# One layer of a diffusion backbone: the attention's probabilities turned and scaled by one product with a diagonal, and the w_o splits ordered behind w_pa's

## The chip, the cores and the metric

The kernel runs on one core of one Trainium2 chip. The metric is the device time of one execution in microseconds. Before the change it is 1527.29 us (median of 3 runs, 1526.62 to 1529.53).

## The reference, cut to what matters

One layer: a half-step SwiGLU feed-forward, then two mixers side by side (a two-dimensional neighbourhood attention and a bidirectional gated DeltaNet), merged by per-channel gates, then a second feed-forward. There are 512 latent tokens, 256 context tokens, a model width of 1024 and 8 attention heads of width 64; everything is float32. The attention of one head over one row of the grid, and the merge:

```python
s = jnp.concatenate([s_loc.reshape(bsz, n_heads, width, n_loc), s_ctx], axis=-1).astype(jnp.float32)
p = jax.nn.softmax(s, axis=-1).astype(v.dtype)
...
return (jnp.einsum('bhwij,bhiwjd->bhwd', p_loc, v_win)
        + jnp.einsum('bhwn,bhnd->bhwd', p[..., n_loc:], v_ctx))
...
y = jax.nn.sigmoid(gate_a) * (o_a @ w_pa) + jax.nn.sigmoid(gate_b) * (o_b @ w_pb)
return y @ w_o
```

So the probabilities are exponentials divided by their row's sum, and they are multiplied with the values. The kernel needs them with the keys on the partitions for that product, so it turns each 128x128 block of them.

## The kernel before, in words

Large products are made of three passes of a rounded format: each operand is split into a high part (a cast on ScalarE, ACT, line 135) and a low part (a subtraction on VectorE, DVE, line 137), both in `split`; the product sums high by high, high by low and low by high (lines 190 to 192, and 209 in `down`). Weights come through a `Stream`: `fill` issues a load on SyncE's queue (line 172), makes the two parts with `split`, and keeps them in a queue; `get` fills a number of weights ahead and hands out the oldest. A stream may carry a table `behind`: for a weight named in it, the cast and the subtraction are issued after two given instructions of the same engines (`tc.issue_after`); it is an order on the engine, not an event to wait for.

The order of instructions on each engine is made by a planner in the tile framework: it runs through the program's order, but puts instructions ahead of others by costs and due times of its own. Each engine then works strictly in that order.

The attention (`attend`, lines 1228 to 1271) runs over 4 pairs of heads m, and in each over 4 column blocks b. For a block, 12 products make the scores of both heads into a PSUM tile `sc` (line 1240; two such tiles); DVE adds the bias (1242) and takes the negated maximum (1244); ACT makes the exponentials into `pr` with their sums `sm` (1248; two tiles of `pr`); DVE takes the reciprocal of the sums (1249). GpSimd (POOL) then multiplies the exponentials of each head with its inverse sums, 128x512 in place (1251). TensorE (PE) turns them, four transposes of 128x128 for each head into a PSUM tile `pt` (1255; two tiles), a set of four below; ACT copies each set into SBUF as `pT` (1257). Then 8 products of the values with `pT` sum into `po` (1266), an ordinary f32 product. At the start of each head pair the values are turned too (`att_values`, 1224 and 1225). Between the blocks stand pieces of other work: `between` calls at eight places the product of the other branch with w_pb (`gated`, lines 1282 to 1288, with 1302), and in the last pair fills four weights of w_o. `att_load` (1163 to 1180) loads and splits queries and keys of the next pair: the casts on ACT (1169), the subtractions on POOL (1170).

The merge (lines 1330 to 1335) runs over 8 column tiles m: it fills w_o up to a number that grows by one in every second step (1331); `gated` takes the weight of w_pa, with one weight ahead, loads the gate `gt` (1285) and makes 12 products; DVE gates the result (1333), POOL adds it to the other branch (1334), and `split` makes the two parts `yh` and `yl`. The product with w_o follows in `down` (209), for four token tiles over all eight tiles of w_o.

Of the kernel before, what the change touches and what calls it, by code (L numbers as in the profile page):

```python
# [10 lines left out]
F32 = mybir.dt.float32  # L11
F32R = mybir.dt.float32r
AF = mybir.ActivationFunctionType
ALU = mybir.AluOpType
# [4 lines left out]
P = 128  # L19
D = 1024  # L20
KT = D // P
# [37 lines left out]
def body(ctx, tc, I, out, dbg=None):  # L59
    nc = tc.nc  # L60
    V, S, G, T = nc.vector, nc.scalar, nc.gpsimd, nc.tensor
    dbg = dbg or {}

    def pool(name, side="left", space=None):
        kw = dict(name=name, bufs=1, reuse_waits="tile")
        if space is not None:
            kw["space"] = space
        else:
            kw["side"] = side
        g = tc.tile_pool(**kw)  # L70
        st = ExitStack()
        p = st.enter_context(g)
        return p, st.close
# [3 lines left out]
    def tl(p, shape, tag, bufs=1, dt=F32):  # L77
        uid[0] += 1
        return p.tile(list(shape), dt, name=f"{tag}_{uid[0]}", tag=tag, bufs=bufs)
# [11 lines left out]
    ident = ident_t[:]  # L91
# [40 lines left out]
    def split(src, hi, lo, behind=()):  # L132

        with tc.issue_after(behind[0]) if behind else nullcontext():
            S.copy(hi, src)  # L135
        with tc.issue_after(behind[1]) if behind else nullcontext():
            V.tensor_tensor(lo, src, hi.bitcast(F32), ALU.subtract)  # L137

    def to_u(tp, pp, xn, uh, ul, c0, scale, shift, tag="u32"):

# [13 lines left out]
    class Stream:  # L154
# [7 lines left out]
        def fill(self, n):  # L162
            while len(self.q) < n and self.i < len(self.srcs):
                src, p, bufs, rp, rb = self.srcs[self.i], self.wp, self.bufs, self.wp, self.bufs
                if isinstance(src, tuple):
                    if src[1] not in self.extra:
                        return
                    p, bufs, rp, rb = self.extra[src[1]]
                    src = src[0]
                c = src.shape[-1]  # L170
                raw = self.raw() if self.raw else tl(rp, [P, D], "wr", rb)
                nc.sync.dma_start(raw[:, 0:c], src)
                hi = tl(p, [P, D], "wh", bufs, F32R)
                lo = tl(p, [P, D], "wl", bufs, F32R)
                split(raw[:, 0:c], hi[:, 0:c], lo[:, 0:c], self.behind.get(self.i, ()))
                self.q.append((hi, lo))
                self.i += 1

# [4 lines left out]
    def mm3(ps, wh, wl, uh, ul, nk=KT):  # L183

        for k in range(nk):
            mm3k(ps, wh, wl, uh, ul, k, nk)
# [133 lines left out]
    def raw1():  # L320
        raws[0] += 1
        k = raws[0] % (5 if more[0] else 3)
        return tl(more[0], [P, D], "wr", 2) if k > 2 else tl(wx, [P, D], "wr") if k == 0 else tl(wp, [P, D], "wr", WB)
# [13 lines left out]
    def rows(w, ks):  # L337
        return [w[k * P:(k + 1) * P, :] for k in ks]
# [26 lines left out]
    def order1():  # L365
        t = lambda fs: [I["up1"][2 * f + j] for f in fs for j in range(2)]
        dn = lambda a, b: rows(I["dn1"], range(a, b))
        o = t(range(F0, F1)) + t(range(F1)) + t(range(F1, HF)) + dn(0, HF) + dn(0, HF - 2)
        o += t(range(HF, NF)) + dn(HF, NF - 4)
        n = len(o)  # L370
        o += dn(HF, NF - KL1)
        o = [(w, "x") if j % 3 == 2 else w for j, w in enumerate(o)]
        return o[:n] + [(w, "tail") for w in dn(NF - 4, NF)] + o[n:]
# [57 lines left out]
    ws = Stream(wp, order1(), WB, 1)  # L431
# [3 lines left out]
    for t in range(2):  # L435
        raw = raw1()
# [99 lines left out]
    def between(j):  # L536
        if j in FIN1:
            t = FIN1.index(j)
            u2(fc, pp, "x", t, finish1(fc, "x", t, accx[t]))
# [16 lines left out]
    src = [I["wab"] if n == "ab" else I["w" + n][m] if n in ("pa", "pb") else I["win"][WIN_IDX[(n, m)]] for n, m in order]  # L556
# [15 lines left out]
    gad = tl(dp, [8, P, NX], "gad")  # L572
    gbd = tl(dp, [8, P, NX], "gbd")

    ws = ws2
    names = iter(order)

    def win_w(name, m):
        assert next(names) == (name, m)
        return ws.get()  # L580
# [628 lines left out]
    oah = tl(np_, [P, 4, NX], "oah", 1, F32R)  # L1209
    oal = tl(np_, [P, 4, NX], "oal", 1, F32R)  # L1210
# [3 lines left out]
    na_, close_na = pool("na")  # L1214

    def att_values(w):

        wf = w[:].rearrange("p b r c -> p b (r c)")
        vw = tl(na_, [P, 4, 2, P], "vw", 2)
        for hb in range(2):  # L1220
            ps = tl(pg, [P, 4, P], "pt", 2)
            for q in range(4):
                b, kt = hb * 2 + q // 2, q % 2
                T.transpose(ps[:, q, :], wf[:, b, kt * P:(kt + 1) * P], ident)
            V.tensor_copy(vw[:, hb * 2:hb * 2 + 2].rearrange("p b k c -> p (b k) c"), ps[:])
        return vw

    def attend(m, qa, ka, kc, bias, w, between):
        vc = tl(na_, [P, 2, P], "vc", 2)
        nc.sync.dma_start(vc[:], vcd[m])  # L1230
        po = tl(pg, [P, 4, P], "po", 1)
        for b in range(4):
            pts = []

            sc = tl(pg, [P, 2, 512], "sc", 2)
            for o, k in ((0, [t.rearrange("p (r c) -> p r c", c=64)[:, :, NA_C0[b]:NA_C0[b] + 32] for t in ka]), (256, kc)):
                for j, (u, v) in enumerate(((0, 0), (0, 1), (1, 0))):
                    for i in range(2):
                        r = slice(i * 64, i * 64 + 64)
                        last = T.matmul(sc[:, i, o:o + 256], qa[u][r, b * P:(b + 1) * P], k[v][r], start=j == 0, stop=j == 2, tile_position=(i * 64, 0))  # L1240
            between(m, b, last.ins)
            V.tensor_tensor(sc[:, :, 0:256], sc[:, :, 0:256], bias[:, (0, 1, 1, 2)[b]], ALU.add)
            nm = tl(na_, [P, 2], "nm", 4)
            V.tensor_reduce(nm[:], sc[:], AX, ALU.max, negate=True)
            pr = tl(na_, [P, 2, 512], "pr", 2)
            sm = tl(na_, [P, 2], "sm", 4)
            for i in range(2):
                S.activation(pr[:, i], sc[:, i], AF.Exp, bias=nm[:, i:i + 1], accum_out=sm[:, i:i + 1])
            V.reciprocal(sm[:], sm[:])
            for i in range(2):  # L1250
                G.tensor_scalar(pr[:, i], pr[:, i], sm[:, i:i + 1], None, op0=ALU.mult)
            for i in range(2):
                pt = tl(pg, [P, 4, P], "pt", 2)
                for q in range(4):
                    T.transpose(pt[:, q, :], pr[:, i, q * P:(q + 1) * P], ident)  # L1255
                pT = tl(na_, [P, 4, P], "pT", 4)
                S.copy(pT[:], pt[:])
                pts.append(pT)
            if b == 0:
                vw = att_values(w)  # L1260

            for q in range(4):
                for i, pT in enumerate(pts):
                    f = slice(i * 64, i * 64 + 64)
                    vv = vw[:, b, q, f] if q < 2 else vc[:, q - 2, f]
                    T.matmul(po[f, b, :], vv, pT[:, q, :], start=(q == 0), stop=(q == 3), tile_position=(0, i * 64))  # L1266
        oa = tl(na_, [P, NX], "oa", 2)
        V.tensor_copy(oa[:].rearrange("p (r b c) -> p r b c", b=4, c=16), po[:].rearrange("p b (r c) -> p r b c", c=16))
        if "oa" in dbg:
            nc.sync.dma_start(dbg["oa"][:, m], oa[:])  # L1270
        split(oa[:], oah[:, m], oal[:, m])
# [10 lines left out]
    def gated(name, gd, m, oh, ol):  # L1282
        wh, wl = win_w(name, m)
        gt = tl(np_, [P, NX], "gt", 2)
        nc.sync.dma_start(gt[:], gd[m])
        ps = tl(pm, [P, NX], *PMB)
        mm3(ps[:], wh, wl, oh, ol, 4)
        return gt, ps
# [15 lines left out]
    for m in range(4):  # L1304
        if m == 3:
# [5 lines left out]
            wso = Stream(wp, [(w, k) if k else w for w, k in zip(rows(I["w_o"], range(KT)), ("b", "b", "b", "b", "o", "o", "o", ""))], WB, 1)  # L1311
# [16 lines left out]
    wo, close_wo = pool("wo", "right")  # L1328
    wso.extra["o"] = (wo, 3, np_, 2)
    for m in range(8):  # L1330
        wso.fill(min(4 + (m + 1) // 2, 7))
        gt, ps = gated("pa", gad, m, oah, oal)
        V.scalar_tensor_tensor(gt[:], gt[:], 1.0, ps[:], op0=ALU.add, op1=ALU.mult)
        G.tensor_tensor(yb[:, m], yb[:, m], gt[:], ALU.add)
        split(yb[:, m], yh[:, m], yl[:, m])
# [80 lines left out]
    src = [I["up2"][i] for i in range(2 * NH)]  # L1416
    ws = Stream(wp, [(w, key(j)) if key(j) else w for j, w in enumerate(src)], WB, 2)
# [134 lines left out]
    ws = Stream(wp, [(w, "d") if j % 6 > 1 else w for j, w in enumerate(rows(I["dn2"], range(NF)))], WB, 2)  # L1552
    ws.extra = {"d": (wd, 4, wp, WB)}
    raw = hs[NH:]
# [8 lines left out]
    for t in range(4):  # L1563
        h = tl(lp, [P, D], "h4", 2)
        n, m = (512, D) if t < 3 else (D // PIECES, 512)
# [125 lines left out]
```

## Time and profile before

| | |
|---|---|
| median of the runs | 1527.29 us (1526.62 to 1529.53) |
| the profiled execution | 1530.66 us, span 1528.8 us |
| granted TensorE clock, mean | 0.988 |
| busy: PE, DVE, ACT | 1462.6, 1050.0, 605.4 us |
| HBM read, written | 206.33 MB, 22.85 MB |

A row of a group reads: line, engine, operation, tile written and tiles read (moving operand first, weights second for a product), shapes, count, then busy time and mean duration in ns, then the idle time of the engine just before and what ended it. A row of the timeline reads: start, duration, engine, line, operation, tiles, count, and in brackets the idle time before it with what ended it. Times count from the start of the span. Matmuls are pipelined and their ends are modelled, so the spacing of starts tells more than the durations.

### The profile page before, as it was taken

How to read it: one execution, taken by the hardware profiler on the slowest of the kernel's cores; microseconds unless marked ns; L12 is line 12 of the kernel's file. 1: busy time of each engine (PE TensorE's matmuls, PEld its weight loads, DVE VectorE, ACT ScalarE, POOL GpSimd, SP SyncE). 2: the span in 40 equal slices, each digit the busy share in tenths (PEclk: the TensorE clock that was granted, in tenths of full speed). 3: DMA queues.
4: the chain of work that ended last, by engine and by line, in shares of the span. 5: the costliest groups of instructions: out<-in, count | busy, mean ns of one | idle time of the engine just before them, and what ended most of it. 6: DMA issues, size and time to landing. Idle time of an engine off the chain costs nothing.

```text
span 1528.8 us, 23646 instructions
## 1 busy us (share of the span) xinstructions
PE 1462.6 (96%) x9221; PEld 1258.7 (82%) x9221; DVE 1050.0 (69%) x1792; ACT 605.4 (40%) x1005; POOL 226.8 (15%) x224
## 2 busy tenths in 40 slices
PE   6999999999999999999996899999999999999997
PEld 4779988888888887889875778867678999998886
DVE  8765942597554587768777895576669699886426
ACT  5444221322222255546543444266416444344310
POOL 0000000000000011323301001366421022220001
PEclk9999999999999999999998999999999999999999
DMA  9665742667454334222476634283353143333422
GB/s 370 207 237 180 222 142 97 211 213 260 168 192 146 130 112 137 87 90 79 141 216 180 172 99 122 69 284 117 91 174 138 56 139 102 106 110 139 138 83 83
DMA packets 107586, 230.72 MB, mean 151 GB/s; under 512 B 34177, under 2 KB 47825, under 8 KB 107473
## 3 DMA queue, kind: packets, MB, share of 16 engines
q1 hardware_dynamic: 105312, 221.79, 44.7%
q10 hardware_dynamic: 1586, 5.32, 0.9%
q0 software_dynamic: 576, 2.10, 0.4%
q8 instruction: 72, 1.18, 0.3%
q14 instruction: 40, 0.33, 0.1%
HBM read 206.33 MB, written 22.85 MB: 150 GB/s over the span
## 4 chain that ended last, share of the span: by engine, by line
PE 76%; DVE 10%; DMA 7%; issue 3%; ACT 2%; POOL 2%; SPq 0%; DVEq 0%; ACTq 0%; POOLq 0%
PE ps L209 19%; PE ps L190 8%; PE ps L192 8%; PE ps L191 8%; PE pm L190 5%; PE pm L192 5%; PE pm L191 5%; PE pc L857 2%; PE ps L1478 2%; PE ps L1480 2%; PE ps L1479 2%; DVE wl L137 2%; PE po L1266 1%; DMA T<-rd 1%; PE pt L1255 1%
## 5 line engine op out<-in xcount | busy, mean ns | idle before, releaser
L137 DVE TENSOR_TENSOR wl<-wr,wh 128x1024 fp32r<-128x1024 f32 (+1 forms) x215 | 263.0, 1228 | 195.1 <-ACT wh L135 194.3
L135 ACT CAST wh<-wr 128x1024 fp32r<-128x1024 f32 (+1 forms) x215 | 217.8, 1018 | 333.4 <-PE ps L209 105.0
L192 PE MATMUL ps<-uxh,wl 128*128 128x512 f32 (+1 forms) x496 | 179.6, 363 | 2.2 <-DVE wl L137 2.2
L191 PE MATMUL ps<-uxl,wh 128*128 128x512 f32 (+1 forms) x496 | 179.3, 363 | 0.8 <-DVE uxl L137 0.8
L190 PE MATMUL ps<-uxh,wh 128*128 128x512 f32 (+1 forms) x496 | 179.6, 365 | 0.0
L279 DVE SCALAR_TENSOR_TENSOR adap<-wr,crow 128x1024 f32<-128x1024 f32 x112 | 136.8, 1221 | 38.5 <-DMA wr<-in_w_adaT_dram 37.1
L112 POOL TENSOR_TENSOR rs<-ve,mhalf 128x1 f32<-128x1 f32 (+2 forms) x46 | 50.4, 1099 | 744.6 <-DVE ve L108 735.4
L190 PE MATMUL pm<-uxh,wh 128*128 128x512 f32 x320 | 133.0, 416 | 4.1 <-ACT spill L609 2.1
L192 PE MATMUL pm<-uxh,wl 128*128 128x512 f32 x320 | 128.2, 401 | 0.7 <-DVE wl L137 0.7
L191 PE MATMUL pm<-uxl,wh 128*128 128x512 f32 x320 | 127.8, 399 | 0.0
L192 PEld LDWEIGHTS ps<-uxh,wl 128*128 128x128 f32 x496 | 93.7, 189 | 17.9 <-DVE wl L137 3.3
L191 PEld LDWEIGHTS ps<-uxl,wh 128*128 128x128 f32 x496 | 94.0, 189 | 14.9 <-DVE uxl L137 1.0
L190 PEld LDWEIGHTS ps<-uxh,wh 128*128 128x128 f32 x496 | 93.4, 189 | 14.3 <-issue 0.8
L190 PE MATMUL ps<-uch,wh 128*128 128x256 f32 x352 | 98.6, 280 | 0.0
L192 PE MATMUL ps<-uch,wl 128*128 128x256 f32 x352 | 98.3, 279 | 0.0
L191 PE MATMUL ps<-ucl,wh 128*128 128x256 f32 x352 | 98.2, 279 | 0.0
L209 PE MATMUL ps<-wh,hx 128*128 128x512 f32 x352 | 94.8, 389 | 0.0
L209 PEld LDWEIGHTS ps<-wh,hx 128*128 128x128 f32 x352 | 65.9, 188 | 13.6
L190 PEld LDWEIGHTS pm<-uxh,wh 128*128 128x128 f32 x320 | 61.6, 193 | 16.3 <-ACT spill L609 3.0
L192 PEld LDWEIGHTS pm<-uxh,wl 128*128 128x128 f32 x320 | 61.7, 193 | 14.8 <-DVE wl L137 1.5
L191 PEld LDWEIGHTS pm<-uxl,wh 128*128 128x128 f32 x320 | 61.6, 192 | 10.6
L190 PEld LDWEIGHTS ps<-uch,wh 128*128 128x128 f32 x352 | 66.1, 188 | 0.6
(411 smaller groups left out, 3438.7 us busy)
## 6 DMA issues: line engine op xcount, KB each, us to landing
wr<-in_w_adaT_dram SPq DMA_DIRECT2D x88, 512.0 KB, 4.7
wr<-in_up_dram SPq DMA_DIRECT2D x80, 512.0 KB, 4.2
wr<-in_dn_dram SPq DMA_DIRECT2D x58, 512.0 KB, 3.5
wr<-in_win_dram SPq DMA_DIRECT2D x52, 512.0 KB, 3.9
rb<-in_up_dram SPq DMA_DIRECT2D x18, 512.0 KB, 3.7
wr<-in_w_o_dram SPq DMA_DIRECT2D x8, 512.0 KB, 4.0
ac<-in_up_dram SPq DMA_DIRECT2D x6, 512.0 KB, 5.2
Dt<-gcd SPq DMA_DIRECT2D x12, 256.0 KB, 5.1
```

What stands on the lines that cost most here:

```text
L112: G.tensor_tensor(rs[:], ve[:], mhalf[:, 0:n], ALU.pow)
L135: S.copy(hi, src)
L137: V.tensor_tensor(lo, src, hi.bitcast(F32), ALU.subtract)
L190: T.matmul(ps, a, uh[:, k, :], start=(k == 0), stop=False)
L191: T.matmul(ps, a, ul[:, k, :], start=False, stop=False)
L192: T.matmul(ps, b, uh[:, k, :], start=False, stop=(k == nk - 1))
L209: T.matmul(banks[t][d][:, c0:c1], a[:, sl], b[:, d * 512 + c0:d * 512 + c1], start=first and j == 0, stop=last and j == 2)
L279: V.scalar_tensor_tensor(pr[:], raw[:], 1.0, crow, op0=ALU.mult, op1=ALU.mult, accum_out=col[:, c:c + 1])
L857: last[0] = T.matmul(*a, **k).ins
L1478: T.matmul(ps[:], a, uh[:, k], start=k == 0, stop=False)
L1479: T.matmul(ps[:], a, ul[:, k], start=False, stop=False)
L1480: T.matmul(ps[:], b, uh[:, k], start=False, stop=k == 3)
```

## The change

Two edits. In the attention, POOL's multiplication goes; DVE makes for each head a diagonal matrix of the inverse sums (identity times the column of inverse sums, 128x128), and the transpose of the exponentials becomes an ordinary f32 product of the exponentials, as weights, with that diagonal as the moving operand. In the merge, the fill of w_o is moved behind `gated` in the program's order, and every cast and subtraction of w_o from there on is to be issued after those of the w_pa weight loaded last; for that, `split` returns its two instructions and the stream keeps them.

```diff
     def split(src, hi, lo, behind=()):
 
         with tc.issue_after(behind[0]) if behind else nullcontext():
-            S.copy(hi, src)
+            a = S.copy(hi, src).ins
         with tc.issue_after(behind[1]) if behind else nullcontext():
-            V.tensor_tensor(lo, src, hi.bitcast(F32), ALU.subtract)
+            b = V.tensor_tensor(lo, src, hi.bitcast(F32), ALU.subtract).ins
+        return a, b
...
-                split(raw[:, 0:c], hi[:, 0:c], lo[:, 0:c], self.behind.get(self.i, ()))
+                self.last = split(raw[:, 0:c], hi[:, 0:c], lo[:, 0:c], self.behind.get(self.i, ()))
...
             V.reciprocal(sm[:], sm[:])
+
+            dg = tl(na_, [P, 2, P], "dg", 2)
             for i in range(2):
-                G.tensor_scalar(pr[:, i], pr[:, i], sm[:, i:i + 1], None, op0=ALU.mult)
+                V.tensor_scalar(dg[:, i], ident, sm[:, i:i + 1], None, op0=ALU.mult)
             for i in range(2):
                 pt = tl(pg, [P, 4, P], "pt", 2)
                 for q in range(4):
-                    T.transpose(pt[:, q, :], pr[:, i, q * P:(q + 1) * P], ident)
+                    T.matmul(pt[:, q, :], pr[:, i, q * P:(q + 1) * P], dg[:, i], start=True, stop=True)
...
     for m in range(8):
+        gt, ps = gated("pa", gad, m, oah, oal)
+
+        wso.behind = {j: ws.last for j in range(KT)}
         wso.fill(min(4 + (m + 1) // 2, 7))
-        gt, ps = gated("pa", gad, m, oah, oal)
         V.scalar_tensor_tensor(gt[:], gt[:], 1.0, ps[:], op0=ALU.add, op1=ALU.mult)
```

## The prediction

> **What bounds the kernel now.** I read the profile page first (busy shares, then the chain), then the table of windows for the two stretches that the change touches, then groups, waits and single rows inside them.
>
> ```profile
> PE 1462.6 (96%) x9221; PEld 1258.7 (82%) x9221; DVE 1050.0 (69%) x1792; ACT 605.4 (40%) x1005; POOL 226.8 (15%) x224
> ...
> PE 76%; DVE 10%; DMA 7%; issue 3%; ACT 2%; POOL 2%; SPq 0%; DVEq 0%; ACTq 0%; POOLq 0%
> ```
>
> TensorE is busy almost throughout and is three quarters of the chain that ends last; GpSimd, from which the change takes its work, is 2% of that chain.
>
> ```profile
> 994.00:1093.45 99.45, 91.86 (x729) 69.36 (x729) 63.42 (x91) 62.49 (x141) 63.75 (x41) 0.97 0.50 171
> 1093.45:1119.52 26.07, 23.30 (x98) 17.66 (x97) 21.35 (x24) 11.67 (x17) 9.79 (x7) 1.00 0.48 151
> 1028.00:1041.00 13.00, 10.33 (x61) 7.74 (x59) 5.77 (x9) 6.32 (x16) 6.74 (x5) 0.74 0.53 180
> 1060.02:1082.51 22.49, 22.49 (x169) 16.93 (x168) 17.19 (x24) 14.78 (x31) 14.93 (x9) 1.00 0.43 141
> ```
>
> The columns are stretch, length, busy PE, PE weight loads, DVE, ACT, POOL (with counts), granted clock, DMA share, GB/s. The first stretch is the attention (first scores to the first w_pa product), the second the merge. In the attention PE is idle for 99.45 - 91.86 = 7.6 us; DVE, ACT and POOL each have about a third of their time free. In 1060 to 1082, most of the last head pair, PE is never idle. Around 1034 there is the one bad place: the granted clock averages 0.74 there.
>
> **Edit 1, the turning.** Line 1251 (POOL) goes and line 1255 changes from a transpose to a product of the same shape, f32 by f32. The question is whether the shape sets the price or the mode.
>
> ```profile
> L1251 POOL TENSOR_SCALAR pr<-pr,sm 128x512 f32<-128x512 f32 x32 | 53.4, 1680 | 28.8 <-DVE sm L1249 23.4 <-PE pt L1224 5.3
> L1255 PE MATMUL pt<-ident,pr 128*128 128x128 f32 x128 | 21.4, 293 | 1.3 <-POOL pr L1251 1.3
> ```
>
> The same stretch of the windows for line 1266 alone:
>
> ```profile
> 994.00:1093.45 99.45, 23.21 (x256) 16.49 (x256) 0.97 0.50 171
> ```
>
> There are 16 blocks (4 head pairs by 4 column blocks). Line 1255 runs 8 times a block, 128 in all, and the trace has 128 records. Line 1266, an ordinary f32 product, also runs 8 times a block, 128 in all, and has 256. So a transpose is one pass of the array as recorded and an f32 product is two. The new line 1255 should have 256 records.
>
> What a record costs, by its start and the start of the next row:
>
> ```profile
> 1017.53 0.60 PE L1255 MATMUL pt<-ident,pr 128*128 128x128 f32 x4
> 1017.89 0.48 PE L191 MATMUL pm<-obl,wh 128*128 128x512 f32 x1
> ...
> 1018.89 0.66 PE L1255 MATMUL pt<-ident,pr 128*128 128x128 f32 x4
> 1019.48 0.54 PE L1266 MATMUL po<-pT,vw 128*64 128x128 f32 x5
> ```
>
> ```profile
> 970.48 1.05 PE L857 MATMUL pc<-r,Tt 128*128 128x128 f32 x8
> 971.37 1.06 PE L857 MATMUL pc<-S,qT 128*128 128x128 f32 x8
> 972.18 0.48 PE L190 MATMUL pm<-uxh,wh 128*128 128x512 f32 x1
> ```
>
> Four transposes take 0.36 us ahead of a 512-wide product and 0.59 us ahead of a product of another tile shape. Four f32 products of 128x128 by 128x128 (eight records, in the scan before) take 0.89 and 0.81, that is (0.89 + 0.81) / 16 = 0.106 us a record. The change adds 128 records: 128 x 0.106 = 13.6 us of PE. The bounds come from pairing the rows the other ways: 32 sets at 0.81 - 0.59 = 0.22 give 7.0, 32 at 0.89 - 0.36 = 0.53 give 17.0. I take 13.6, since both kinds of neighbour occur and the step per record is the same before both.
>
> The Trainium skill, "TensorE: Matmul & The Clock Gate", section Terms, says that transpose mode is four times faster for FP32; "Perfetto Trace Analysis", section Transposes, asks that logical transposes use the transpose and not a standard matmul. By that factor, an estimate from the page, each product would cost four times 0.09 us and the sum would be near +35 us; by that rule a set would take 1.44 us, and the scan's sets of 0.81 and 0.89 do not bear it out.
>
> **What hides it.** Nothing but PE's own idle time, since PE works in order. That time in the attention, by releaser:
>
> ```profile
> PE po L1266 <- ACT pT L1257: 4.0, 5, 1.9
> PE pt L1255 <- POOL pr L1251: 1.3, 2, 0.7
> PE pt L1224 <- DVE vw L1225: 0.8, 1, 0.8
> PE sc L1240 <- ACT pr L1248: 0.7, 1, 0.7
> ...
> PE sc L1240 <- POOL ka L1170: 0.2, 1, 0.2
> ```
>
> Only 1.5 us of it names POOL: 1.3 for the scaled probabilities, and 0.2 for a split (line 1170) queued behind them on POOL. Both should go. The scores wait for exponentials, not for POOL, so the 53.4 us taken from POOL are mostly time that nobody waits for.
>
> Behind 1.8 of the 4.0 us stands POOL indirectly: in the last two blocks there is no other work left and the sets come as late as POOL delivers them.
>
> ```profile
> 1088.28 0.54 PE L1266 MATMUL po<-pT,vw 128*64 128x128 f32 x5 [0.37 <-ACT pT L1257]
> ...
> 1090.68 0.43 PE L1266 MATMUL po<-pT,vw 128*64 128x128 f32 x2 [0.73 <-ACT pT L1257]
> ...
> 1092.43 0.54 PE L1266 MATMUL po<-pT,vw 128*64 128x128 f32 x5 [0.73 <-ACT pT L1257]
> ```
>
> With the diagonal ready within a microsecond of the reciprocal, the sets can be issued back to back and the copies of pT hide behind the next set; I give 1.5 of the 1.8 back. Late next is the copy after the last set.
>
> The rest of the 4.0 is the bad place at 1034:
>
> ```profile
> 1032.25 0.62 ACT L1169 CAST kah<-ka 128x512 fp32r<-128x512 f32 x1 [4.01 <-DMA ka<-kad]
> ...
> 1034.25 0.58 ACT L1257 COPY pT<-pt 128x512 f32<-128x512 f32 x1
> ```
>
> ```profile
> 1034.88 0.90 PE L1266 MATMUL po<-pT,vw 128*64 128x128 f32 x5 [1.88 <-ACT pT L1257]
> ...
> 1036.78 1.12 PE L1255 MATMUL pt<-ident,pr 128*128 128x128 f32 x4
> 1037.82 0.58 PE L1240 MATMUL sc<-kah,qah 64*128 64x256 f32 x2
> ```
>
> ACT waits 4.0 us at the head of its queue for the keys of the last head pair, with the pT copy queued behind; PE stands 1.9 us and then runs at half clock: a set takes 1.04 instead of 0.59. A mean clock of 0.74 over 13.00 us is half clock for 2 x 0.26 x 13.00 = 6.8 us, a loss of 3.4, of which the 1.9 us of standing take 0.9; so 2.5 us of work are lost besides the wait. The wait is for a DMA, not for POOL, and stays; the two sets that PE has just ahead of it grow by 0.8 us and eat into it, and the half clock may or may not follow. I take half of 1.9 + 2.5: 2.2 us. Given back in all: 1.5 + 1.5 + 2.2 = 5.2 us. The bounds are 0 and all idle time plus the half clock, 7.6 + 2.5 = 10.1.
>
> **The diagonal.** It adds two DVE operations a block, 32 in all, queued behind the reciprocal and ahead of the next block's bias add.
>
> ```profile
> L685 DVE TENSOR_SCALAR na<-na x7: 181/188/190, 690.7 to 699.0; 128x48 f32<-128x48 f32 x7
> ...
> L998 DVE COPY Y<-pi x6: 271/281/283, 833.1 to 951.7; 128x128 f32<-128x128 f32 x6
> ```
>
> Not in the trace before; between 0.19 (smaller, same operation) and 0.28 (same size, out of PSUM) each, so 6 to 9 us on DVE, 36 us of which are free in the stage. DVE also gains: beside POOL's operations its two-input subtractions take up to 1.75 us instead of 0.68 (a row of 1.75 is below). I cost it at nothing; if the cover were gone, each block's chain would be 0.4 to 0.6 us longer against 3.4 us (two of 1680 ns) that leave it with POOL.
>
> **Edit 2, the casts.** In the merge PE waits 2.7 us in all, for the low halves of w_pa:
>
> ```profile
> 1101.42 0.50 PE L192 MATMUL pm<-oah,wl 128*128 128x512 f32 x1 [0.95 <-DVE wl L137]
> ...
> 1114.18 0.50 PE L192 MATMUL pm<-oah,wl 128*128 128x512 f32 x1 [1.78 <-DVE wl L137]
> ```
>
> ```profile
> 1094.81 2.00 ACT L135 CAST wh<-wr 128x1024 fp32r<-128x1024 f32 x2
> 1098.54 1.14 ACT L135 CAST wh<-wr 128x512 fp32r<-128x512 f32 x2 [1.73 <-PE pm L191]
> ```
>
> ```profile
> 1095.88 2.36 DVE L137 TENSOR_TENSOR wl<-wr,wh 128x1024 fp32r<-128x1024 f32 x2 [0.26 <-ACT wh L135]
> ...
> 1111.17 0.69 DVE L1333 SCALAR_TENSOR_TENSOR gt<-gt,pm 128x512 f32<-128x512 f32 x1 [1.00 <-DMA gt<-gad]
> 1111.77 0.69 DVE L137 TENSOR_TENSOR yl<-yb,yh 128x512 fp32r<-128x512 f32 x1
> 1112.38 1.75 DVE L137 TENSOR_TENSOR wl<-wr,wh 128x512 fp32r<-128x512 f32 x1
> ```
>
> Rows of 1024 are w_o, rows of 512 w_pa. Two of w_o's splits run at 1094.8 to 1098.2, when ACT and DVE have nothing else: the next w_pa cast cannot start before 1098.54, because its buffer is still being read by PE. They delay nobody. The 1.78 us wait has no w_o split ahead of it at all, but the gate's DMA (1.00), a yl, and a subtraction stretched to 1.75. So binding w_o behind w_pa takes away little: the issue of the gate load ahead of w_o on SP may be worth a few tenths. Against that, two splits of 2.36 us on DVE leave an idle stretch for a busy one (21.35 of 26.07). Bounds -2.7 and +2.4; I take 0, because w_o's next use is after all eight w_pa products.
>
> **The sum.** 13.6 - 5.2 + 0 = +8.4 us. The profiled execution took 1530.66 (span 1528.8), 3.4 above the median of 1527.29; on it 1539.1, on the median 1535.7.
>
> **The rivals.**
> - No change: PE loses all its idle time. 13.6 - 10.1 - 2.7 = +0.8, 1528. For it: the idle time is there. Against: half of it follows a DMA, and single waits of this order at tile hand-overs return in any order of work. 0.14.
> - Faster: the second record of a product is nearly free, because its weight load or stream overlaps the first's in this mix of short products. It decides below 5.2 / 128 = 0.04 us a record; at 0.02 the sum is 2.6 - 5.2 = -2.6, at zero 1522. For it: no row has this product between po and score products. Against: 0.106 in the scan. 0.16.
> - The bound casts become the wait: DVE's 2.4 us land ahead of w_pa's subtractions. 8.4 + 2.4 = +10.8, 1538. For it: DVE at 82% in the merge. 0.13.
> - The rule of four passes: three more passes of 0.09 for 128 products, 35 - 5 = +30, 1557. As a mechanism it is that each of the two records takes twice the pass; the scan's rows speak against. 0.02.
> - The forecast, 0.55.
>
> **How the numbers follow.** A measurement of this kernel can tell about 0.2%, 3 us, from no change. Slower holds the forecast, the bound casts and the four passes, 0.70; same 0.14; faster 0.16. The range: upwards 17.0 for the records with 1.3 + 0.5 given back, about +15.5, so 1543; downwards the no-change case and the upper part of the faster one, 1525.
>
> **What would show it.** Line 1255 with 256 records and about 0.8 to 1.0 us a set; PE busy up by some 13 us in the attention, idle below 5; POOL near 63.75 - 53.4 = 10 us there; the last set's wait the only one of the tail; the w_o splits after w_pa's in the merge and that stretch near 26 us. I am wrong if line 1255 keeps 128 records or its records cost under 0.04 us, if the attention is not longer than 99.5 us, or if the merge shortens by over 2 us.

## The result and the profile after

The changed kernel takes 1541.65 us (median of 6 runs, 1537.77 to 1545.04). The kernel before, run beside it, takes 1527.22 us (6 runs, 1525.69 to 1529.53). The ratio is 1.009 with a 95% interval of 1.0071 to 1.0108: slower by 14.4 us. The forecast was 1535.7 with a range from 1525 to 1543, slower with a chance of 0.70.

One warning about the two profiles. The profiled execution of before took 1530.66 us, 3.4 above its median; that of after took 1537.77, the fastest of its six. So the two traces differ by 7.1 us where the medians differ by 14.4. The stages were therefore compared over several profiles of each kind, below.

The page of after, the busy times and the shares of the chain that ended last:

```profile
PE 1476.1 (96%) x9349; PEld 1275.0 (83%) x9349; DVE 1055.4 (69%) x1824; ACT 605.2 (39%) x1005; POOL 174.7 (11%) x192
...
PE 78%; DVE 11%; DMA 5%; issue 2%; POOL 1%; ACT 1%; SPq 0%; DVEq 0%; POOLq 0%; ACTq 0%
```

PE has 9349 - 9221 = 128 more records and 13.5 us more busy time; POOL has lost 32 instructions and 52 us. TensorE's share of the chain rose from 76% to 78%.

The windows of after for the attention, the merge, and the stretch from the first product with w_o to the first product of the last stage (the sums of seven products in the second feed-forward), with the columns of before:

```profile
992.07:1100.79 108.72, 104.91 (x857) 84.60 (x856) 69.11 (x123) 62.33 (x141) 9.82 (x9) 1.00 0.47 157
1100.79:1128.42 27.63, 23.68 (x98) 17.62 (x97) 23.69 (x25) 11.69 (x17) 11.40 (x7) 1.00 0.44 138
1128.42:1222.30 93.88, 92.47 (x609) 84.64 (x608) 69.61 (x110) 42.10 (x76) 13.67 (x14) 1.00 0.37 128
```

The attention grew from 99.45 to 108.72 us: 13.05 us more busy PE (91.86 to 104.91), less 3.8 us of idle time (7.6 to 3.8). The merge grew from 26.07 to 27.63. The third stretch became shorter; in the profile of before it is

```profile
1119.52:1217.10 97.58, 94.54 (x609) 86.17 (x608) 72.22 (x111) 42.03 (x76) 14.25 (x14) 0.98 0.35 122
```

that is 97.58 against 93.88 us. Keep this row in mind for the second edit.

The turning line of after, by source line:

```profile
L1258 PE MATMUL pt<-dg,pr x256: 270/275/377, 1000.2 to 1098.8; 128*128 128x128 f32 x128
```

256 records for 128 products, each of a transpose's length. PE's timeline in the third head pair shows what a set of four now takes, by its start and the start of the next row:

```profile
1042.44 1.16 PE L1258 MATMUL pt<-dg,pr 128*128 128x128 f32 x8
1043.53 0.38 PE L1241 MATMUL sc<-kah,qah 64*128 64x256 f32 x2
...
1048.39 1.16 PE L1258 MATMUL pt<-dg,pr 128*128 128x128 f32 x8
1049.30 0.48 PE L193 MATMUL pm<-obh,wl 128*128 128x512 f32 x1
...
1097.89 1.16 PE L1258 MATMUL pt<-dg,pr 128*128 128x128 f32 x8
1098.97 0.43 PE L1269 MATMUL po<-pT,vw 128*64 128x128 f32 x2
1099.78 0.54 PE L1269 MATMUL po<-pT,vw 128*64 128x128 f32 x5 [0.37 <-ACT pT L1260]
```

A set takes 1.09 us ahead of a product of another tile shape (before: 0.59) and 0.91 ahead of a 512-wide one, where the four single sets of after take 0.81 to 0.92. Before, the three sets ahead of a 512-wide product took 0.36, 0.41 and 0.42; the prediction shows the shortest, and this is the middle one:

```profile
1015.22 0.66 PE L1255 MATMUL pt<-ident,pr 128*128 128x128 f32 x4
1015.63 0.47 PE L191 MATMUL pm<-obl,wh 128*128 128x512 f32 x1
```

So a set costs about 0.50 us more before either neighbour, 32 times. The last two of the rows of after are the tail: the copy of the last set is now the only wait there, 0.37 us, where before three waits of 0.37, 0.73 and 0.73 stood in the last two blocks.

PE's waits in the attention of after:

```profile
PE sc L1241 <- ACT pr L1249: 1.6, 1, 1.6
PE pt L1225 <- ACT pT L1260: 1.3, 1, 1.3
PE pt L1258 <- DVE dg L1254: 0.5, 1, 0.5
PE po L1269 <- ACT pT L1260: 0.4, 1, 0.4
```

No wait names POOL any more. The 4.0 us of the value products (line 1266, now 1269) for `pT` are down to 0.4. One wait of 0.5 for the new diagonal has come, and two have grown: that of the scores for exponentials from 0.7 to 1.6, and that of the values' turning for `pT` from 0.3 to 1.3. In the merge DVE now does this:

```profile
1102.28 0.69 DVE L137 TENSOR_TENSOR oal<-oa,oah 128x512 fp32r<-128x512 f32 x1 [0.69 <-ACT oah L135]
1106.11 1.28 DVE L1338 SCALAR_TENSOR_TENSOR gt<-gt,pm 128x512 f32<-128x512 f32 x2 [3.14 <-PE pm L193]
1107.31 4.22 DVE L137 TENSOR_TENSOR wl<-wr,wh 128x512 fp32r<-128x512 f32 x3
```

DVE stands still for 3.14 us at the place where it made two subtractions of w_o before (2.36 us at 1095.88). The w_o parts come later, among w_pa's.

### The profile page after: what moved, and what is told of

Its sections match the earlier page's. It is cut to its first block, busy times and chain, and to the rows that moved or that the text cites. A ratio compares the mean times of both kernels' runs of the same rounds, so it can differ in the third digit from the quotient of the medians.

```text
span 1536.0 us, 23873 instructions
## 1 busy us (share of the span) xinstructions
PE 1476.1 (96%) x9349; PEld 1275.0 (83%) x9349; DVE 1055.4 (69%) x1824; ACT 605.2 (39%) x1005; POOL 174.7 (11%) x192
## 4 chain that ended last, share of the span: by engine, by line
PE 78%; DVE 11%; DMA 5%; issue 2%; POOL 1%; ACT 1%; SPq 0%; DVEq 0%; POOLq 0%; ACTq 0%
PE ps L210 19%; PE ps L191 9%; PE ps L193 9%; PE ps L192 9%; PE pm L191 5%; PE pm L193 5%; PE pm L192 5%; PE pc L858 3%; PE pt L1258 2%; PE ps L1485 2%; PE ps L1483 2%; PE ps L1484 2%; DVE wl L137 2%; PE po L1269 1%; DMA Dt<-gcd 1%
## 5 line engine op out<-in xcount | busy, mean ns | idle before, releaser
L191 PEld LDWEIGHTS ps<-uxh,wh 128*128 128x128 f32 x496 | 92.7, 188 | 14.4 <-issue 0.8
L193 PE MATMUL ps<-uch,wl 128*128 128x256 f32 x352 | 98.3, 279 | 0.0
L210 PEld LDWEIGHTS ps<-wh,hx 128*128 128x128 f32 x352 | 65.9, 188 | 13.6
```

What stands on the lines that cost most here:

```text
L191: T.matmul(ps, a, uh[:, k, :], start=(k == 0), stop=False)
L193: T.matmul(ps, b, uh[:, k, :], start=False, stop=(k == nk - 1))
L210: T.matmul(banks[t][d][:, c0:c1], a[:, sl], b[:, d * 512 + c0:d * 512 + c1], start=first and j == 0, stop=last and j == 2)
```

## The experiments

**Theory A**: the second record of each product is the loss, at a higher price in this mix of short products than in the scan; POOL's step gives a few microseconds back; the casts are worth little. **Rival B**: the bound casts in the merge are a substantial part of it. **Rival C**: the products themselves are cheap, and the loss comes from the other order that the planner makes, and from the diagonals on DVE. Times are medians; each ratio is to runs of the kernel before on the same chip.

### The first edit alone

```diff
+            dg = tl(na_, [P, 2, P], "dg", 2)
             for i in range(2):
-                G.tensor_scalar(pr[:, i], pr[:, i], sm[:, i:i + 1], None, op0=ALU.mult)
+                V.tensor_scalar(dg[:, i], ident, sm[:, i:i + 1], None, op0=ALU.mult)
...
-                    T.transpose(pt[:, q, :], pr[:, i, q * P:(q + 1) * P], ident)
+                    T.matmul(pt[:, q, :], pr[:, i, q * P:(q + 1) * P], dg[:, i], start=True, stop=True)
```

> Edit 1 alone, the fill of w_o where it was. Theory A (the second record of each f32 product is the price): +9 to +15 us over the kernel before, the attention about as long as with both edits, 108.7 us. Rival B (the bound w_o splits are the price): within 3 us of the kernel before. Rival C (the planner's new order around DVE's diagonals is the price): near the whole loss too, so this run does not tell A from C.

Measured: 1538.87 us against 1527.62, ratio 1.0075 (1.0056 to 1.0093), +11.2 us. Its windows for attention and merge:

```profile
993.83:1102.85 109.02, 104.94 (x858) 84.62 (x857) 69.14 (x123) 62.42 (x141) 9.82 (x9) 1.00 0.46 156
1102.85:1128.58 25.73, 23.30 (x98) 17.66 (x97) 21.36 (x24) 11.67 (x17) 9.90 (x7) 1.00 0.48 149
```

The attention is that of the whole change (108.72); the merge is that of before (26.07). Most of the loss is the first edit's, and the longer merge is the second's.

### The second edit alone

The diff is the second edit: `split` returns its two instructions, the stream keeps them, and the merge loop has the moved fill and the line `wso.behind = {j: ws.last for j in range(KT)}`.

> Edit 2 alone, the attention as before. A: -1 to +2 us, the merge 26 to 28 us long. B: +8 to +14 us.

Measured: 1526.02 us against 1527.62, ratio 0.9987 (0.9978 to 0.9996), -1.6 us. Its windows for attention, merge, the stretch behind it, and 40 us that begin 60 us into that stretch and reach a little past its end:

```profile
992.83:1091.33 98.50, 90.71 (x729) 68.69 (x728) 62.30 (x91) 62.60 (x141) 63.57 (x41) 0.98 0.52 173
1091.33:1118.96 27.63, 23.65 (x98) 17.65 (x97) 23.69 (x25) 11.57 (x17) 11.39 (x7) 1.00 0.43 139
1118.96:1212.80 93.84, 92.52 (x610) 84.69 (x609) 69.72 (x110) 42.16 (x76) 13.69 (x14) 1.00 0.37 128
1178.96:1218.96 40.00, 37.41 (x313) 36.63 (x311) 28.56 (x44) 20.56 (x36) 2.32 (x2) 1.00 0.19 65
```

and the same 40 us (60 to 100 us after the first product with w_o) of before:

```profile
1179.52:1219.52 40.00, 37.86 (x310) 37.66 (x309) 26.81 (x44) 18.14 (x34) 0.67 (x2) 0.96 0.23 79
```

The merge loses 27.63 - 26.07 = 1.6 us and the next stretch gains 97.58 - 93.84 = 3.7: the granted clock in the 40 us is 1.00 instead of 0.96, PE's wait for `y` (line 128) is 1.3 us instead of 2.1, and a wait of 0.8 for `uxl` (line 137) is gone. So rival B falls as the main cause: alone the second edit is a small gain, made of two opposite effects. What this experiment doesn't say is whether it is the move or the binding; see the move without the binding, below.

### The product alone, with the identity

```diff
-                    T.transpose(pt[:, q, :], pr[:, i, q * P:(q + 1) * P], ident)
+                    T.matmul(pt[:, q, :], pr[:, i, q * P:(q + 1) * P], ident, start=True, stop=True)
```

> The kernel before with one thing changed: the transposes are ordinary f32 products with the identity, GpSimd still scales. A: line 1255 has 256 records, 0.8 to 1.1 us a set, and the kernel is 12 to 19 us slower, more than with the whole change, since GpSimd's step is still in the chain of each block. C: 0 to 4 us, since nothing new is queued on DVE.

Measured: 1543.49 us against 1527.62, ratio 1.01 (1.0084 to 1.0116), +15.9 us. Its window of the attention:

```profile
993.20:1106.97 113.77, 108.83 (x858) 87.51 (x857) 64.48 (x91) 63.32 (x141) 61.07 (x41) 0.97 0.44 150
```

In the program nothing but the kind of instruction has changed, and POOL still scales; line 1255 has 256 records, a set takes 1.09 us ahead of a product of another tile shape, and the attention grows by 113.77 - 99.45 = 14.3 us. That is the price of 128 products for 128 transposes: 0.112 us each by the stage, 0.124 by the medians (0.100 to 0.138 by their interval). The planner's order of PE's work is not quite that of before (between the first two sets stand 4 score products instead of 8), and this price contains what that does.

### POOL's step left out

```diff
-            for i in range(2):
-                G.tensor_scalar(pr[:, i], pr[:, i], sm[:, i:i + 1], None, op0=ALU.mult)
```

> The kernel before without GpSimd's scaling, transposes kept (the division by the sums is left out of the attention). It prices what the change takes away: A expects -2 to -6 us, the idle time that names GpSimd, the tail and part of the half clock around 1034 us. If the step is worth nothing, within 1 us; if it is worth as much as it looks by its 53 us busy, below -10 us.

Measured: 1522.97 us against 1527.62, ratio 0.9969 (0.9957 to 0.9982), -4.65 us.

```profile
991.14:1086.87 95.73, 89.63 (x729) 67.44 (x729) 60.30 (x91) 62.52 (x141) 9.69 (x9) 0.98 0.54 178
```

The attention is shorter by 99.45 - 95.73 = 3.7 us, and POOL's busy time by 54 us. So this is all that the step on POOL costs when it goes without a replacement. It is not simply the waits that go: PE's idle time in the stage falls only from 7.6 to 6.1 us, and its busy time, with the clock at 0.98 instead of 0.97, by 2.2 us. The waits for POOL are gone and those of the value products for `pT` are 0.8 instead of 4.0, but two others have come in their place, of which before had 0.3 us:

```profile
PE pt L1224 <- ACT pT L1255: 2.6, 1, 2.6
PE pm L190 <- ACT spill L607: 2.6, 1, 2.6
```

With the product by the identity the sum closes: +15.9 - 4.65 = +11.25, and the first edit alone measured +11.2. Each of the three is known to 2 or 3 us only, so that it closes to a tenth is chance.

### The whole change again

No diff: the changed kernel, on the chip of the next three.

> The changed kernel once more, beside the others of this call. A: +9 to +16 us. The merge should again be 1.5 to 2 us longer than before (27.6 us) and the stretch from the first w_o product to the first product of the seven (93.9 us) 2 to 4 us shorter, as edit 2 alone showed; if the merge is back at 26 us, that reading was chance.

Measured: 1541.62 us against 1526.51, ratio 1.009 (1.0066 to 1.0113), +15.1 us. Its window of the attention, and 17 us early in it:

```profile
994.90:1106.47 111.57, 106.46 (x858) 85.79 (x857) 70.21 (x123) 62.44 (x141) 9.73 (x9) 0.98 0.45 153
...
1003.00:1020.00 17.00, 12.71 (x98) 10.43 (x98) 13.51 (x24) 11.35 (x27) 4.93 (x5) 0.90 1.01 376
```

The result stands, and so do the longer merge (27.62 us) and the shorter stretch behind it (93.81). The attention is 2.9 us longer than in the first profile of the same kernel: early in it PE waits 2.9 us for exponentials instead of 1.6, and the clock falls to 0.90. The 16 DMA engines are full here (1.01), but they were as full at the same place of the first profile, where the clock stayed at 1.00:

```profile
1000.00:1017.00 17.00, 13.87 (x117) 11.50 (x119) 13.83 (x25) 12.34 (x30) 4.95 (x5) 1.00 1.04 394
```

So what makes the difference is not shown, and one profile of this stage is worth no more than about 3 us.

### The first edit in the rounded format

On top of the first edit, the exponentials and the diagonal are tiles of the rounded format that the large products of this kernel use, so that the same product takes one pass:

```diff
-            pr = tl(na_, [P, 2, 512], "pr", 2)
+            pr = tl(na_, [P, 2, 512], "pr", 2, F32R)
...
-            dg = tl(na_, [P, 2, P], "dg", 2)
+            dg = tl(na_, [P, 2, P], "dg", 2, F32R)
```

> Edit 1 alone, but exponentials and diagonal in the rounded format that the large products use, so that the turning keeps DVE's diagonals and the order around them, and only the passes per product differ (the probabilities lose low bits). A: line 1257 has 128 records, 0.4 to 0.6 us a set, and the kernel is 1 to 6 us faster than before, near the run without the scaling. C (order, diagonals on DVE): still 8 us or more slower.

Measured: 1526.11 us against 1526.51, ratio 0.9999 (0.9988 to 1.0009), -0.4 us. Its window of the attention:

```profile
991.59:1089.20 97.61, 93.07 (x730) 72.97 (x729) 68.79 (x123) 62.53 (x141) 10.76 (x9) 0.95 0.50 175
```

and PE's timeline:

```profile
1021.28 0.66 PE L1257 MATMUL pt<-dg,pr 128*128 128x128 f32 x4
1021.78 0.44 PE L192 MATMUL pm<-obh,wl 128*128 128x512 f32 x1
...
1023.17 0.66 PE L1257 MATMUL pt<-dg,pr 128*128 128x128 f32 x4
1023.76 0.39 PE L1240 MATMUL sc<-kah,qah 64*128 64x256 f32 x2
```

Four records a set and 0.59 us ahead of a product of another tile shape, as with the transposes of before; ahead of a 512-wide product 0.50 us, a little more than their 0.36 to 0.42. The diagonals on DVE are there, POOL is freed, the planner has the same operations to order; the second record is gone, and with it the loss of 11 us. This is what tells theory A from rival C. The planner's order did change with it (after the first value products two sets follow each other, where the first edit alone has one and then waits for exponentials), so taken alone this run would leave something of C. But the spacing of the sets was read where they stand, between the same kinds of neighbours, and 32 times 0.50 us is the price that the product by the identity measured: C falls. The forecast of 1 to 6 us faster was missed: it is not faster than before by the 4.65 us of POOL's step left out. The granted clock is 0.95 here, against 0.97 before and 0.98 there.

### The scaling on DVE, and with the second edit

If POOL's step costs 4.65 us and the products cost 15.9, the step can go to DVE and the transposes can stay:

```diff
-                G.tensor_scalar(pr[:, i], pr[:, i], sm[:, i:i + 1], None, op0=ALU.mult)
+                V.tensor_scalar(pr[:, i], pr[:, i], sm[:, i:i + 1], None, op0=ALU.mult)
```

> Transposes kept, the scaling of 128x512 on DVE in place of GpSimd, nothing else changed. A: 1 to 5 us faster than before, since GpSimd's step leaves the chain and PE gets no work. Rival (DVE takes GpSimd's place as the wait): within 1 us or slower.

Measured: 1524.1 us against 1526.51, ratio 0.9988 (0.9972 to 1.0004), -2.4 us. Its window of the attention, and then the line:

```profile
994.27:1092.54 98.27, 92.10 (x730) 70.06 (x729) 75.08 (x123) 62.21 (x141) 10.24 (x9) 0.95 0.52 173
```

```profile
L1251 DVE TENSOR_SCALAR pr<-pr,sm x32: 473/480/1340, 1002.2 to 1088.1; 128x512 f32<-128x512 f32 x32
```

DVE takes 0.48 us (median) for what took POOL 1.56 (1.68 in the mean), and its busy time in the stage rises from 63.42 to 75.08 of 98.27 us. With the second edit beside it:

> As the run with the scaling on DVE, with edit 2 as well. If the two gains add, 1 to 2 us faster than with DVE's scaling alone, 3 to 6 us faster than before; if the longer merge comes through, equal or slower than DVE's scaling alone.

Measured: 1522.81 us against 1526.51, ratio 0.9986 (0.9972 to 1.0), -3.7 us; merge 27.67, the stretch behind it 93.88. Both medians are under the kernel before, but both intervals reach 1.0. The clock is 0.95 in both attentions. By the reckoning of the prediction (half clock for twice the missing share, half of that lost) 0.95 over 98.3 us loses 4.9 us and 0.97 over 99.5 us loses 3.0. The difference of 1.9, an estimate, is about what DVE's scaling stays behind POOL's step left out (2.4 against 4.65). The intervals of those two overlap, though, and the profiled execution of DVE's scaling took 1529.55 us, 5.4 above its median, so this alone shows little. The clock over all runs points the same way: its mean over the whole execution is 0.9875 in the first edit in the rounded format, 0.9877 and 0.9883 in these two, and 0.9892 in the 29 runs of the kernel before on the same chip. By the same reckoning that is 1.3 to 2.5 us, an estimate.

### The move without the binding

The second edit without `wso.behind = {j: ws.last for j in range(KT)}`: the fill only stands behind `gated`.

> The kernel before with only the first half of edit 2: the fill of w_o stands behind the w_pa product in the program, but its casts are not bound. If the binding moves the two w_o splits out of their idle stretch, the merge is near 26 us here and the stretch behind it 96 to 98 us, as before; if the move in the program does it, 27.6 and 93.9 us, as with edit 2.

Measured: 1528.25 us against 1527.14, ratio 1.0007 (0.9992 to 1.0022). Its windows for the merge and the stretch behind it:

```profile
1092.80:1118.70 25.90, 23.26 (x97) 17.67 (x97) 21.41 (x24) 11.68 (x17) 9.85 (x7) 1.00 0.47 149
1118.70:1215.40 96.70, 93.86 (x609) 85.84 (x608) 72.12 (x111) 42.07 (x76) 14.18 (x14) 0.98 0.35 124
```

25.90 and 96.70: nearly those of before. Both effects of the second edit, the longer merge and the shorter stretch behind it, belong to the binding.

### The first edit alone, a second time

> Edit 1 alone once more. Both edits took 1541.6 us twice, edit 1 alone 1538.9 with a wide interval. If edit 2 costs beside edit 1, this comes out near 1539 again, 11 us over the kernel before; if it gives its 1.6 us there too, near 1543.

Measured: 1539.65 us against 1527.14, ratio 1.0079 (1.0061 to 1.0098), +12.5 us. Its window of the attention:

```profile
997.79:1109.60 111.81, 106.47 (x857) 85.69 (x856) 70.23 (x123) 62.45 (x141) 9.74 (x9) 0.98 0.46 153
```

The profiled execution took 1546.62 us, 7.0 above its median. The longer form of the attention (111.57 when the whole change ran again) comes without the second edit too, so it isn't the casts' doing.

### Both, and the first edit alone, side by side

The whole change had measured 2 to 3 us above the first edit alone, where the second edit alone is 1.6 faster than before; they had never been timed side by side.

> The whole change once more, on the same chip as the first edit alone, since these two were never timed side by side. Theory 1 (the second edit is worth its 1 to 2 us gain beside the first edit too, and the difference seen so far is chance): this kernel comes out 1 to 2 us under the first edit alone, near 1538. Theory 2 (the second edit costs beside the first, through the waits for the sums sn in the last stage): 2 to 3 us above it, near 1541.5, with PE waits on sn of about 2 us again and 313.6 us from the first product of the last stage to the end of the span.

> The first edit alone, on the same chip as the whole change. Both theories: 1539 (1538.9 and 1539.7 were measured), 311.8 us from the first product of the last stage to the end, no PE wait on sn. What tells them apart is the difference to the whole change: above it by 1 to 2 us by theory 1, below it by 2 to 3 us by theory 2.

Measured: the whole change 1540.55 us, ratio 1.008 (1.0066 to 1.0094); the first edit alone 1539.11, ratio 1.007 (1.0056 to 1.0084), both against 1527.56. The difference of 1.4 us lies between the two theories' values, with intervals that overlap. The last stage, from its first product to the end, of the whole change:

```profile
1224.40:1538.10 313.70, 300.75 (x1934) 272.12 (x1932) 219.30 (x301) 109.63 (x153) 48.63 (x34) 0.99 0.33 110
```

and of the first edit alone:

```profile
1227.00:1538.80 311.80, 302.09 (x1934) 274.57 (x1932) 218.93 (x301) 110.60 (x153) 49.22 (x34) 0.99 0.33 110
```

PE's waits for the sums `sn` there, of the whole change (the first edit alone has none):

```profile
PE ps L1483 <- DVE sn L1504: 1.2, 1, 1.2
PE ps L1483 <- DVE sn L1505: 1.1, 2, 0.8
PE ps L1483 <- DVE sn L1507: 0.8, 2, 0.6
```

In three profiles of the whole change this stage takes 313.6 or 313.7 us, with such waits in each; in three of the first edit alone 311.7 or 311.8, with none. That is the second theory's mark. Between these two profiles the merge is 1.9 us longer (27.66 against 25.74), the stretch behind it 3.6 shorter (93.99 against 97.54) and the last stage 1.9 longer, together 0.3 us; so these stages don't account for the 1.4 us of the medians either. And the waits do not settle the length: the profile of before has 1.9 us of the same waits at 311.7, the first edit in the rounded format and the move without the binding have 313.3 us without the whole second edit, and the second edit alone has 311.7 us and no such wait. So the longer stage goes with the whole change here, and what puts the stage into the one course or the other stays open.

## Why the prediction was right or wrong

**Direction and mechanism: right.** The product with the diagonal is two records, and the second is not hidden; line 1258 has its 256. In the profile after, PE's busy time in the attention rose by 13.05 us (13.6 was forecast), idle time fell to 3.8 (below 5), POOL to 9.82 (10), no wait names POOL, and the last copy is the only wait of the tail. In the five other profiles with the first edit in f32 the idle time was 3.0 to 5.3 us. That the busy time rose by so nearly the 13.6 of the forecast is luck: before, it contains the 2.5 us that the prediction reckoned as lost to the half clock, and after, at a clock of 1.00, it doesn't; 13.05 + 2.5 = 15.6 us, an estimate, is what the records cost.

**The price of the records: mis-sized, 13.6 for 15.9.** The prediction took 0.106 us a record from sets of the scan that stand one behind the other, and said the step per record is the same before both kinds of neighbour. The step that failed is taking that mean of a set, 0.106, for the price of an added record. The step is nearly the same before both neighbours, as it said, but higher: a set in the attention takes 0.50 us more than the transposes it replaces (1.09 for 0.59, and 0.91 for 0.41), that is 0.125 for each of the four records added, and not 0.106. 32 x 0.50 = 16.0 is what the product by the identity measured (15.9, with an interval of 12.8 to 17.7, which alone would not exclude 13.6). The scan's 0.81 is a set ahead of a 512-wide product; three of the attention's four single sets of that kind take 0.91 or 0.92. The bounds, 7.0 to 17.0, held it. In the range, the upper sum 17.0 - 1.3 - 0.5 is 15.2 and not 15.5, which changes nothing.

The Trainium skill, "TensorE: Matmul & The Clock Gate", section Terms, gives transpose mode as four times faster for FP32. The runs disagree for this shape: a set of products against a set of transposes is 1.09 to 0.59 us and, at the middle, 0.91 to 0.41, so 1.8 to 2.2 times.

**What is given back: near in sum, 5.2 for 4.65, and not in its parts.** The run with POOL's step left out measures this term alone: of 53.4 us of POOL's work, 4.65 us were on the path (2.8 to 6.6 by its interval). The stages agree: +14.3 for the products and -3.7 for POOL's step make +10.6 in the attention, and the six profiles with the first edit in f32 show +9.3, +9.6, +12.1, +12.4, +10.0 and +9.6, +10.5 in the mean. The 99.45 us of before are one profile; the same attention took 98.50 and 99.07 us in the second edit alone and in the move without the binding. In the profile after, the 1.5 us that named POOL went as forecast, and of the 1.8 us of the tail 1.5, as forecast. At the bad place ACT still waits for the keys of the last head pair, as forecast (3.70 us ahead of the cast `kah` at 1035.03). But PE no longer waits behind it, and no half clock follows: of 1.9 + 2.5 us I gave half back, and all of it went. Against that, the prediction had no term for waits that come or grow elsewhere, here 0.5 us for the diagonal and 1.9 more for exponentials and for `pT`. So the nearness of the sum is in part luck. The clock of the attention was 1.00 in three of the six profiles and 0.98 in the other three, against 0.97.

**The diagonal: right.** 0.28 us each (its median duration by the source line), the upper bound, and hidden but for a wait of 0.5 us (0.3 to 1.0 in the six profiles):

```profile
L1254 DVE TENSOR_SCALAR dg<-ident,sm x32: 276/280/753, 999.9 to 1094.5; 128x128 f32<-128x128 f32 x32
```

**The casts: near zero for a wrong reason.** "They delay nobody" was true of the place that the w_o splits left, not of the one they went to. In the merge the binding cost 1.6 to 1.9 us, so that the stretch was not near 26 us but 27.6, and PE waits 3.9 us there instead of 2.7:

```profile
PE pm L193 <- DVE wl L137: 3.2, 3, 1.7
PE pm L191 <- ACT wh L135: 0.7, 1, 0.7
```

That is the rival of the bound casts (2.4), as a mechanism; it was named, and given 0.13. What I did not see at all is the gain behind it, 3.0 to 3.7 us in the stretch that follows. The search for who gains should have gone past the stage in which the casts are moved.

**The remainder.** The miss is 14.4 - 8.4 = 6.0 us. 2.3 of it is the records and 0.5 what was given back. The other 3.2 are the second edit beside the first, where I had 0, and no run explains them in full: the whole change measured +14.4, +15.1 and +13.0 us over the kernel before beside it, the first edit alone +11.2, +12.5 and +11.6, and side by side they differ by 1.4 us. The one to two microseconds beyond that are within the interval of the result, which reaches from 10.8 to 16.5 us. Where in the kernel the 1.4 us arise stays open.

## What to carry to other kernels

A 128x128 f32 transpose that becomes an ordinary f32 product got a second record here and cost about half a microsecond more per set of four; where TensorE is the bound, a multiplication folded into it in that way must free more than that from the path. What a step on another engine is worth is measured by who waits for it, not by its busy time: 53 us on POOL were worth 4.65. Such a scaling is better tried on the engine that does it in 0.48 us, with the transposes left as they are (here a gain of 2.4 us that is not clear of the noise), and a reordering should be followed into the next two stages before it is booked at nothing.

## What the runs showed of the hardware

The granted clock in the attention was 1.00 or 0.98 in the six profiles with the first edit in f32, 0.97 before and with the product by the identity, 0.98 with POOL's step left out, and 0.95 in the three kernels that moved POOL's scaling to DVE and kept one record a turn. So freed time does not all arrive: by the reckoning above, those three lost about 2 us to the clock that the kernel before does not lose. In all three the low clock lies in the first 30 us of the attention, with a mean of 0.83, and the next 65 us run at 1.00. PE is idle for 3.7 to 4.9 us of those 30; but the first edit alone has 3.7 us of idle time in its first 30 us at a clock of 1.00, so the sum of the idle time does not decide it. What in their order of work lets the clock fall was not tried.
